# The last two experts behind the static norm, and one test of the list lengths where three were nested

## The chip, the cores and the metric

The kernel runs on one core of one Trainium2 chip. The metric is the device time of one launch in microseconds, from the core's first instruction to its last, as the median of several runs. Beside it stands one execution that the hardware profiler took; all rows of the trace come from that one, and its times count from the start of its span.

## The reference, cut

One decoder layer on 512 tokens of width 1024, in float32. Ahead of what matters here lie a layer norm, a mixer (differential attention and a gated short convolution) and a second norm. Then comes the part that the change touches: 32 experts, of which each token takes two of one group, and the last norm.

```python
def hier_moe(x, w_rg, b_rg, w_re, b_re, w1, w3, w2):
    ...                        # top-1 group, top-2 experts in it, gates
    def expert_block(args):
        xb, e = args
        return (jax.nn.silu(xb @ w1[e]) * (xb @ w3[e])) @ w2[e]
    ...                        # rows sorted by expert, padded, computed, gated
    return jnp.zeros_like(xt).at[tok].add(y).reshape(B, S, D)

# in reference(), after the mixer and its norm
ffn = hier_moe(h, w_rg[l], b_rg[l], w_re[l], b_re[l], w1[l], w3[l], w2[l])
h = layer_norm(DN_ALPHA * h + ffn, ln2_g[l], ln2_b[l])
```

## The kernel before, in words

Tokens lie in four blocks of 128 rows. `acc` (traced as `hres`) holds the four blocks of the sum that the last norm takes, 128 x 4 x 1024. The program goes through the 32 experts in a fixed order. For each of the first 30, `expert_flow(m)` multiplies the gathered rows of that expert with w1 and w3 (`up`, line 1158), applies silu on ScalarE (ACT) and the product on VectorE (DVE), turns the result (`turn`, line 1178 and 1179), multiplies with w2 (`down_products`, line 1191), scales with the gate, and adds the rows of the pair of experts before it to `acc` with selection products (`spread`, lines 1214 and 1216). Rows come in blocks of 32 slots: a first block of every expert is straight code, second to fourth blocks lie behind tests of the expert's count (`n_e`, lines 1339, 1358, 1366, 1374). The third and fourth block, "rest", lie far off the straight path, and `hint()` puts a branch hint for them on TensorE (PE), DVE and ACT behind the first block's products; their test has line 1366. Weights come through a ring of 17 places of 1 MB that SyncE (SP) fills in order (line 672); `place(k)` is the place of the k-th load.

The last two experts, lists of 64 slots at most, are not added to `acc` and normed with all else. The 512 tokens are normed without them ("static norm", written out by SP), and the rows of these two lists are normed a second time with their expert's part and written over the first by an indirect DMA from GpSimd (POOL). The steps by name:

- `summed_half(t, hf, both)` adds experts 28 and 29 to half a block of `acc` and sums it (L1528 on PE, L1530 on DVE); `spread_rows(k)` brings half a row of ln2's gain or shift to all partitions (L1499, copied by ACT, L1500); `squares(t, ...)` gives the variance (L1512, L1513); `rstds` the reciprocal root (L1517, L1518 on ACT, then five instructions on POOL, L1519 to L1523); `shifted_(t)` and `scaled_(t)` make the output rows (L1612, L1615), and SP writes them.
- `Slots(i, few)` is one list: `up`, `silu`, `gated`, `gather` (adds the rows of `acc` to the product's PSUM tile, L1568), `turn`, `down`, then `mean`, `rstd`, `norm` on the row pieces, and `write`. With `few` a list has 32 slots and each row lies in four pieces of 256, else 64 slots and two pieces of 512. `gains_of(n)` cuts ln2's rows to these pieces (L1505).
- `last_two(few, few_)` is the whole ending with both lists, written out four times: for each list in the short or the long form. `longest > 128` (line 1684, the crowded case) is tested first, then list 30 against 32 (line 1764), then list 31 against 32 (line 1765 or 1770). None of the three has a hint. Within `last_two` PE, DVE, ACT and POOL follow the order of the text, in which the sums and rows of the static norm stand between the two experts' products.

For these inputs no list is over 32 slots and none crowded: the trace shows the lines of the fourth copy, behind tests 1684, 1764 and 1770. What sets the order around the change is thus the text of `last_two`, the loads that SP issued up to 1254 us, and what the sequencer of each engine needs to get from the end of `expert_flow(29)` to that copy.

## Time and profile before

| what | value |
|---|---|
| time, median of 3 runs | 1298.69 us (1296.23 to 1305.65) |
| the profiled execution's own time | 1313.07 us |
| its span, first to last instruction | 1311.3 us |
| PE busy (weight loads apart) | 1099.6 us, 84% |
| DVE, ACT, POOL busy | 652.7, 434.2, 325.7 us |
| mean granted PE clock | 0.922 |
| last regular expert's last instruction (DVE) ends | 1254.7 us |
| first instruction of the last two experts on DVE, PE | 1272.1, 1273.4 us |
| last write to the output starts | 1305.2 us |

The page's row of 40 slices has PE at 9 tenths or near it up to the middle, and at 5 to 8 tenths through the experts; the last two slices, 33 us each, have 3 and 5 tenths of PE. The page's chain of waits follows only the last write and says nothing of the end; the timeline and the waits of the last 60 us do.

### The profile page before, as it was taken

Reading aid. Unit: us, or ns where it says so; the run is one execution under the profiler, and the core shown is the slowest. Engines: PE = TensorE matmul, PEld = TensorE weight load, DVE = VectorE, ACT = ScalarE, POOL = GpSimd, SP = SyncE. Lnnn points to the kernel's source line nnn. Section 1 sums busy time; section 2 is a strip of 40 time slices with the busy share of each in tenths; the row PEclk is TensorE's granted clock in tenths of the full one; section 3 lists DMA queues with packets and bytes.
Section 4 is the critical chain, followed back from the end, with each engine's and each line's share of the span. In section 5 each row is a group of like instructions: output and inputs, shape, how many; then the busy total and the mean of one; then the engine's idle time right before and its main releaser. Section 6 shows DMA issues by size and latency. Waiting matters only on the chain. (4 is left out here: it accounts for less than half of the span.)

```text
span 1311.3 us, 22649 instructions
## 1 busy us (share of the span) xinstructions
PE 1099.6 (84%) x8684; PEld 800.7 (61%) x8684; DVE 652.7 (50%) x1320; ACT 434.2 (33%) x953; POOL 325.7 (25%) x243
## 2 busy tenths in 40 slices
PE   7999999999999999998677778766776668787835
PEld 5887877877778888897445545444443445454513
DVE  7356666575666035538653444342454333445426
ACT  4444545455432223315221223121322112222214
POOL 3423333333235444425740201100000000000021
PEclk8999999999999999998798878888898887899968
DMA  6323222322264333584488946999645995685861
GB/s 186 94 74 103 65 79 88 85 70 67 73 175 128 89 83 95 191 322 180 183 329 363 390 169 254 377 366 372 248 194 205 380 400 209 251 352 232 319 254 73
DMA packets 127591, 267.73 MB, mean 204 GB/s; under 512 B 11745, under 2 KB 89930, under 8 KB 111023
## 3 DMA queue, kind: packets, MB, share of 16 engines
q1 hardware_dynamic: 117684, 254.72, 52.6%
q10 hardware_dynamic: 4666, 6.01, 1.4%
q0 software_dynamic: 5056, 4.50, 1.1%
q8 instruction: 121, 1.98, 0.7%
q14 instruction: 64, 0.52, 0.1%
HBM read 272.25 MB, written 4.52 MB: 211 GB/s over the span
## 5 line engine op out<-in xcount | busy, mean ns | idle before, releaser
L136 POOL TENSOR_TENSOR wl<-raw,wh 128x1024 fp32r<-128x1024 f32 x84 | 212.1, 2541 | 339.0 <-ACT wh L135 339.0
L1290 DVE TENSOR_TENSOR first<-p,first 64x256 f32<-64x256 f32 x49 | 20.9, 426 | 244.5 <-ACT first L1289 244.5
L135 ACT CAST wh<-raw 128x1024 fp32r<-128x1024 f32 x84 | 85.9, 1047 | 115.1 <-PE po L368 64.3
L1289 ACT ACTIVATE first<-p 64x256 f32<-64x256 f32 x49 | 18.5, 378 | 290.6 <-PE p L1158 282.3
L1284 DVE SCALAR_TENSOR_TENSOR ysb<-p,gts,ysb 32x256 fp32r<-32x256 f32 x164 | 78.7, 480 | 52.3 <-ACT ysb L1281 46.8
L1158 PE MATMUL p<-ring,xT 128*32 128x256 f32 x752 | 66.8, 461 | 38.4 <-PEq L1366 28.3
L1216 DVE TENSOR_TENSOR hres<-pc,hres 128x512 f32<-128x512 f32 x152 | 92.7, 680 | 6.4 <-PE pc L1214 3.5
L1281 ACT ACTIVATE ysb<-p,gts 32x256 fp32r<-32x256 f32 x164 | 76.5, 466 | 55.8 <-PE p L1191 52.4
L1078 POOL DMA_INDIRECT xgs<-h1d,idxs x15 | 15.4, 1026 | 316.7 <-PE px L1299 315.0
L1158 PE MATMUL p<-ring,first 128*32 128x256 f32 x896 | 66.6, 421 | 30.5 <-PEq L1366 22.0
L1158 PEld LDWEIGHTS p<-ring,xT 128*32 128x32 f32 x752 | 43.8, 131 | 55.6 <-issue 44.8
L1158 PEld LDWEIGHTS p<-ring,first 128*32 128x32 f32 x896 | 45.0, 120 | 47.8 <-issue 31.3
L1191 PE MATMUL p<-ring,first 128*32 128x256 f32 x944 | 59.9, 389 | 4.8 <-ACT first L1179 4.0
L1214 PE MATMUL pc<-ysb,sel 128*128 128x512 f32 x224 | 59.2, 406 | 0.5 <-PEq L1339 0.5
L921 PE MATMUL pd<-wh,mT 128*128 128x256 f32 x256 | 50.0, 296 | 1.2 <-DVE hres L927 1.2
L1158 PE MATMUL p<-ringraw,first 128*32 128x256 f32 x208 | 24.0, 484 | 32.1 <-DVE ysbr L1628 21.3
L368 PE MATMUL pg<-hTH,wh 128*128 128x512 f32 x128 | 50.7, 396 | 0.0
L368 PE MATMUL pg<-hTH,wl 128*128 128x512 f32 x128 | 50.5, 395 | 0.0
L368 PE MATMUL pg<-hTL,wh 128*128 128x512 f32 x128 | 50.5, 395 | 0.0
L457 ACT ACTIVATE e<-e,mn 128x128 f32<-128x128 f32 (+3 forms) x64 | 35.7, 558 | 40.2 <-DVE mn L454 40.0
L1214 PEld LDWEIGHTS pc<-ysb,sel 128*128 128x128 f32 x224 | 39.7, 188 | 14.9 <-issue 6.4
L1179 ACT COPY first<-ph 128x128 f32<-128x128 f32 x51 | 13.6, 266 | 101.7 <-PE ph L1178 101.5
(498 smaller groups left out, 2761.2 us busy)
## 6 DMA issues: line engine op xcount, KB each, us to landing
ring<-in_w_dram SPq DMA_DIRECT2D x114, 1024.0 KB, 11.5
raw<-in_w_in_dram SPq DMA_DIRECT2D x50, 512.0 KB, 4.4
ringwl<-in_w_dram SPq DMA_DIRECT2D x23, 1024.0 KB, 8.9
ringraw<-in_w_dram SPq DMA_DIRECT2D x22, 1024.0 KB, 9.0
ringwh<-in_w_dram SPq DMA_DIRECT2D x22, 1024.0 KB, 13.0
ringh<-in_w_dram SPq DMA_DIRECT2D x11, 1024.0 KB, 15.4
raw<-in_w_in_dram SPq DMA_DIRECT2D x7, 1024.0 KB, 5.5
raw<-in_w_attn_proj_dram SPq DMA_DIRECT2D x8, 512.0 KB, 5.5
```

The source lines that it names most:

```text
L135: A.copy(wh[:, ks], raw[:, ks])
L136: G.tensor_tensor(wl[:, ks], raw[:, ks], wh[:, ks].bitcast(F32), op=ALU.subtract)
L368: T.matmul(out_ps, l[:, k, c0:c0 + P], r[:, k, :], start=k == 0 and i == 0, stop=k == ND - 1 and i == 2)
L457: A.activation(e[:, :w], e[:, :w], AF.Exp, bias=mn[:], scale=-1.0, accum_out=sm)
L921: T.matmul(pds[n], mTs[t // 2][l][:, t % 2, k, :], r[:, k, :], start=k == 0 and i == 0, stop=k == ND - 1 and i == 2)
L1158: one = T.matmul(p1[m * g:m * g + m, 0:wd], xT[:, j, s0:s0 + m], (w1, w3)[2 * g // n][j][:, c0:c0 + wd], start=j == 0, stop=j == ND - 1)
L1191: T.matmul(o, l, r, start=j == 0 and not onto, stop=j == 3)
L1214: T.matmul(pc[:], sel[:, t * P:(t + 1) * P], ys[hf], start=i == 0, stop=i == len(parts) - 1)
L1216: added = V.tensor_tensor(at, pc[:], at, op=ALU.add)
L1281: high = A.activation(h, src, AF.Copy, scale=gc).ins
L1284: lows.append(V.scalar_tensor_tensor(l, src, gc, h.bitcast(F32), op0=ALU.mult, op1=ALU.subtract).ins)
L1290: turns["act"] = V.tensor_tensor(hh, p1[64:128, 0:256], hh, op=ALU.mult), one
```

## The change

The last two experts are written once, each list in blocks of 32 slots. `Slots(i, b)` is now block b of list i, always in four pieces of 256. The nested tests on each list's length go. The sums, spread rows, squares, rstd and gain copies of the static norm are taken out of `last_two`, put ahead of the crowded test and kept in the order of the text on PE, DVE and ACT; `sq` is one buffer of 1024 columns where there were two, and `ob` lies in other places. The crowded test stays and gets a hint, placed on PE behind the first sum's products, on DVE behind that sum, on ACT behind the copy of the rows. Behind it `last_two` does block 0 of both lists in an order of its own, and behind the last write one test (`longer > 32`) leads to block 1 of both. One of three values that were loaded into registers at m = 12 goes. The crowded case adapts (`spread_too`). In the diff below, lines of that case and repeated names are left out.

```diff
-    def expert_flow(m):
+    def expert_flow(m, spread_too=True):
...
-            V.tensor_copy(cmx[:, 1:3], last2)
+            V.tensor_copy(cmx[:, 1:2], mxf[:, 1:2])
...
-        for k, n in enumerate((4, 2)):
-            for g in range(n):
-                m = P // n
-                G.tensor_scalar(idx_[m * g:m * g + m, i, k:k + 1], token[0:m], float(n), float(g), op0=ALU.mult, op1=ALU.add)
+        for b in range(2):
+            for g in range(4):
+                G.tensor_scalar(idx_[32 * g:32 * g + 32, i, b:b + 1], token[32 * b:32 * b + 32], 4.0, float(g),
+                                op0=ALU.mult, op1=ALU.add)
...
-            longest, n_30, n_31 = (nc.values_load(cmx[0:1, i:i + 1], engines=every, min_val=0, max_val=2 * S)
-                                   for i in range(3))
-
-    in_order.__exit__(None, None, None)
+            longest, longer = (nc.values_load(cmx[0:1, i:i + 1], engines=every, min_val=0, max_val=2 * S)
+                               for i in range(2))
...
-    def gains_of(n):
...
+    def gains_of():
+        for g in range(4):
+            A.copy(gains[32 * g:32 * g + 32], g2[32 * g:32 * g + 32, :, 256 * g:256 * g + 256])
...
-        def __init__(self, i, few):
...
+        def __init__(self, i, b):
+            self.i, self.b, self.s0 = i, b, 64 * i + 32 * b
+            self.sel = onehots[:, i, :, 32 * b:32 * b + 32]
+            self.gc = gates_[:, i, b:b + 1]
...
-    ob = [spare_at[4 + t // 2][:, 1024 * (t % 2):1024 * (t % 2) + 1024] for t in range(NT)]
-    sq = spare_at[6]
+    by_hand = dict(engines={ENG.PE, ENG.DVE, ENG.Activation})
...
+    def last_two():
+
+        a_, b_ = Slots(0, 0), Slots(1, 0)
+        with tc.manual_schedule(**by_hand):
+            a_.up()
+            a_.silu()
+            a_.gated()
+            for t in range(NT):
+                shifted_(t)
+            a_.gather()
+            a_.turn()
+            a_.down()
+            b_.up(range(0, 4))
+            b_.gather()
+            exp_tables()
+            a_.mean()
+            a_.rstd()
+            A.preload_act_table_set("silu_and_others")
+            a_.norm()
+            scaled_(0)
+            scaled_(1)
+            b_.up(range(4, ND))
+            b_.silu()
+            b_.gated()
+            scaled_(2)
+            scaled_(3)
+            one = a_.write().ins
+            b_.turn()
+            exp_tables()
+            b_.down()
+            b_.mean()
+            b_.rstd()
+            b_.norm()
+            other = b_.write().ins
+            with tc.If(longer > 32):
+                for i in range(2):
+                    Slots(i, 1).all()
+        tc.declare_no_dep(other, one, reason="the two lists' rows differ")
+
+
+    ob = [place(6 * NE + 1)[:, 1024:2048], spare_at[3][:, 1024:2048]] + [xgs[:, t, :] for t in range(2)]
+    sq = place(6 * NE + 1)[:, 0:1024]
...
-    def last_two(few, few_):
...
-    with tc.If(longest > 128) as crowded:
+
+    copied = A.copy(rows2[0], rows_)
+    V.tensor_tensor(rows2[1], rows_, rows2[0].bitcast(F32), op=ALU.subtract)
+    for t in range(NT):
+        for hf in range(2):
+            added = summed_half(t, hf, both)
+            if t == 0 and hf == 0:
+                hint("crowded", (*added, copied))
+        if t in (0, 2):
+            spread_rows(t)
+            spread_rows(t + 1)
+        squares(t, sq)
+    exp_tables()
+    rstds(slice(0, NT))
+    A.preload_act_table_set("silu_and_others")
+    gains_of()
+    in_order.__exit__(None, None, None)
+
+    with tc.If(longest > 128, label="crowded") as crowded:
         fetch(xgr[:], NE - 1)
...
     with crowded.Else():
-        with tc.If(n_30 > 32) as many:
-            with tc.If(n_31 > 32) as many_:
-                last_two(False, False)
...
+        last_two()
```

Three places in the order of the instructions. ACT between the end of expert 29 and expert 31's silu: before, all of this stands behind the third test (L1770). `p_19118` and `p_19243` are the up products of experts 30 and 31, `first` the activations, `pg` a spread row, `ring_4534` ln2's rows, `hres` is `acc`, `ve` and `y_5587` variance and reciprocal root.

```order
L1627 CAST ysbr<-ring_4535 4x512
L1558 ACTIVATE first<-p_19118 64x256
L1500 COPY ring_4534<-pg 128x512 x2
L1513 ACTIVATE ringwh,ve<-hres,nmu 128x1024 x2
L1500 COPY ring_4534<-pg 128x512 x2
L55 ACT_TABLE_LOAD
L1513 ACTIVATE ringwh,ve<-hres,nmu 128x1024 x2
L1517 ACTIVATE y_5587<-ve,eps_17433 128x4
L1518 ACTIVATE y_5587<-y_5587 128x4
L1179 COPY first<-ph 128x128
L1656 ACT_TABLE_LOAD
L1505 COPY ring_4534<-ring_4534 32x512 x4
```

The same stretch of ACT now:

```order
L1665 CAST ysbr<-ring_4535 4x512
L1787 BRANCH_PREFETCH_HINT
L1494 COPY ring_4534<-pg 128x512 x2
L1506 ACTIVATE ring_4533,ve<-hres,nmu 128x1024 x2
L1494 COPY ring_4534<-pg 128x512 x2
L1506 ACTIVATE ring_4533,ve<-hres,nmu 128x1024 x2
L55 ACT_TABLE_LOAD
L1510 ACTIVATE y_5587<-ve,eps_17421 128x4
L1511 ACTIVATE y_5587<-y_5587 128x4
L1678 ACT_TABLE_LOAD
L1498 COPY ring_4534<-ring_4534 32x512 x4
L1682 COMPARE_AND_BRANCH
```

Expert 30's silu (L1558, now L1549) moved from the second place to behind the test, and all of the norm stands ahead of it. DVE behind the tests, from the last row means on; before, `p_19221` being the sum of expert 30's down product and gathered rows:

```order
L1512 TENSOR_SCALAR nmu<-sm 128x1 x2
L1612 SCALAR_TENSOR_TENSOR ringraw<-hres,nmu,ring_4534 128x1024 x4
L1615 SCALAR_TENSOR_TENSOR ringraw<-ringraw,y_5587,ring_4534 128x1024 x2
L1561 SCALAR_TENSOR_TENSOR first<-p_19243,ring_4535,first 64x256
L1615 SCALAR_TENSOR_TENSOR ringraw<-ringraw,y_5587,ring_4534 128x1024 x2
L1580 BN_STATS ring_4535<-p_19221 128x6
L1581 BN_AGGR ring_4535<-ring_4535 128x2
L1582 TENSOR_SCALAR ring_4535<-ring_4535 128x4
```

And now, from expert 30's gated product (L1552) on, `p_18473` being its up product and `p_18512` the sum of its down product and gathered rows:

```order
L1552 SCALAR_TENSOR_TENSOR first<-p_18473,ring_4535,first 64x256
L1658 SCALAR_TENSOR_TENSOR ring_4533<-hres,nmu,ring_4534 128x1024
L1658 SCALAR_TENSOR_TENSOR ring_4535<-hres,nmu,ring_4534 128x1024
L1658 SCALAR_TENSOR_TENSOR xgs<-hres,nmu,ring_4534 128x1024 x2
L1584 BN_STATS ring_4535<-p_18512 128x6
L1585 BN_AGGR ring_4535<-ring_4535 128x2
L1586 TENSOR_SCALAR ring_4535<-ring_4535 128x4
L1591 BN_STATS ring_4535<-pm 128x6
L1592 BN_AGGR ring_4535<-ring_4535 128x2
L1593 TENSOR_SCALAR ring_4535<-pm,ring_4535 128x1
L1594 SCALAR_TENSOR_TENSOR ring_4535<-p_18512,ring_4535,ring_4534 128x256
```

Expert 30's gated product now stands ahead of the shifted rows, with no sums between, and its statistics and norm follow them at once; before, they stood behind all four scaled rows (L1615), which now come later (L1661). POOL at the program's end, before:

```order
L1519 TENSOR_SCALAR ve<-ve 128x4
L1520 TENSOR_TENSOR u_5588<-ve,y_5587 128x4
L1521 TENSOR_TENSOR u_5588<-u_5588,y_5587 128x4
L1522 TENSOR_SCALAR u_5588<-u_5588 128x4
L1523 TENSOR_TENSOR y_5587<-u_5588,y_5587 128x4
L1604 DMA out_dram<-ring_4535,idx 2048x256 x2
L1770 UNCONDITIONAL_BRANCH
```

And now, from the crowded case's end on:

```order
L1682 UNCONDITIONAL_BRANCH
L1607 DMA out_dram<-ring_4535,idx 2048x256 x2
L1648 COMPARE_AND_BRANCH
L1607 DMA out_dram<-ring_4535,idx 2048x256 x2
L1648 UNCONDITIONAL_BRANCH
```

The rstd instructions moved ahead of the crowded test, and a test stands behind the two writes, over two more.

## Rows read from the trace of the kernel before

**Rows 1.** Waits of 1252 to 1274 us: who waited for whom, total us, times, longest us

```profile
DVE ysbr L1628 <- issue: 17.4, 1, 17.4
...
ACT ysbr L1627 <- issue: 9.0, 1, 9.0
```

**Rows 2.** Stretches: length, busy us per engine (instructions), PE clock, DMA share, GB/s

```profile
1254.86:1272.09 17.23, 0.00 (x0) 0.00 (x0) 0.00 (x0) 0.62 (x1) 5.33 (x17) 0.55 0.71 268
1273.30:1276.80 3.50, 3.43 (x36) 1.84 (x39) 0.00 (x0) 0.00 (x0) 0.00 (x0) 0.50 0.02 5
```

**Rows 3.** Lines of the three tests: ns min/median/max, first and last start us

```profile
L1684 PEldq COMPARE_BRANCH  x1: 7241/7241/7241, 1253.2 to 1253.2; - x1
...
L1764 ACTq COMPARE_BRANCH  x1: 57/57/57, 1257.6 to 1257.6; - x1
...
L1764 DVEq COMPARE_BRANCH  x1: 71/71/71, 1261.2 to 1261.2; - x1
...
L1770 ACTq COMPARE_BRANCH  x1: 45/45/45, 1262.6 to 1262.6; - x1
...
L1770 DVEq COMPARE_BRANCH  x1: 56/56/56, 1267.6 to 1267.6; - x1
```

**Rows 4.** DMA, 1256 to 1264 (packets, MB, share), and issues from 1245 on

```profile
q8 instruction: 4, 0.07, 6.3%
...
ring<-in_w_dram SPq DMA_DIRECT2D x5, 1024.0 KB, 16.9
```

**Rows 5.** Line 1366 (columns as rows 3), and the whole run's waits behind it

```profile
L1366 PEldq COMPARE_BRANCH  x35: 77/468/5582, 642.8 to 1252.5; - x35
...
PE p L1158 <- PEq L1366: 63.7, 15, 7.5
...
ACT first L1289 <- DVEq L1366: 2.4, 3, 0.8
```

**Rows 6.** Timeline of PE: start us, us, instruction, count, idle before

```profile
1273.37 3.64 PE L1158 MATMUL p<-ringraw,first 128*32 128x256 f32 x32 [21.26 <-DVE ysbr L1628]
...
1277.41 1.20 PE L1528 MATMUL pc<-ysb,sel 128*128 128x512 f32 x4
...
1291.21 1.91 PE L1158 MATMUL p<-ring,first 128*32 128x256 f32 x32
```

**Rows 7.** Timeline of ACT

```profile
1281.87 1.08 ACT L1500 COPY ring<-pg 128x512 f32<-128x512 f32 x2 [1.38 <-PE pg L1499]
1282.86 1.15 ACT L1513 ACTIVATE ringwh<-hres,nmu 128x1024 f32<-128x1024 f32 x1
...
1286.69 1.28 ACT L55 ACT_TABLE_LOAD   x1
...
1292.39 2.54 ACT L1505 COPY ring<-ring 32x512 f32<-32x512 f32 x4
```

**Rows 8.** Timeline of DVE

```profile
1286.80 4.87 DVE L1612 SCALAR_TENSOR_TENSOR ringraw<-hres,nmu,ring 128x1024 f32<-128x1024 f32 x4
...
1295.82 2.47 DVE L1615 SCALAR_TENSOR_TENSOR ringraw<-ringraw,y,ring 128x1024 f32<-128x1024 f32 x2
1298.32 0.43 DVE L1580 BATCH_NORM_STATS2 ring<-p 128x6 f32<-128x256 f32 x1
...
1299.77 0.17 DVE L1588 BATCH_NORM_STATS2 ring<-pm 128x6 f32<-128x4 f32 x1 [0.54 <-PE pm L1584]
...
1302.68 0.16 DVE L1588 BATCH_NORM_STATS2 ring<-pm 128x6 f32<-128x4 f32 x1
...
1304.40 0.48 DVE L1601 SCALAR_TENSOR_TENSOR ring<-ring,ring 128x256 f32<-128x256 f32 x1
```

**Rows 9.** Timeline of POOL, and its drains at the end (line 1798)

```profile
1303.06 1.12 POOL L1604 DMA_INDIRECT out_dram<-ring,idx  x1 [10.19 <-DVE ring L1589]
1305.17 0.97 POOL L1604 DMA_INDIRECT out_dram<-ring,idx  x1 [0.99 <-POOLq L1684]
...
L1798 POOLq DRAIN  x3: 46/105/5135, 1305.3 to 1311.0; - x3
```

192 lines of the change are left out of this document (61 added, 131 removed).

## The prediction

> **What bounds the kernel now.** I read the views from the end backwards. The waits of 1252 to 1274 us come first: between the last regular expert and the last two, DVE waits 17.4 us and ACT 9.0, and the view says "issue", that is, for nothing that it knows of [rows 1]. The stretches say the same: from 1254.86 to 1272.09 PE and DVE do nothing and ACT 0.62 us, while DMA moves 268 GB/s [rows 2]. Then the lines of the three tests (1684, 1764, 1770): every engine takes three jumps in a row. DVE leaves the last expert at 1254.9, takes the second test at 1261.2, the third at 1267.6, and works at 1272.1: 6.3, 6.4 and 4.5 us each. On PE the record of the first test itself lasts 7.24 us. ACT takes the second at 1257.6 and the third at 1262.6, 5.0 us apart, and works 0.5 us behind that [rows 3]. In the middle of it the instruction queue moves packets, on DMA engines that are busy with weights [rows 4]. So I read each long jump as a wait for instructions.
>
> Against these stand the skips of a "rest" block, which every expert makes with a branch hint ahead (line 1366). PE's test takes 77 to 5582 ns there, median 468, and PE's experts waited for it for 63.7 us, in 15 waits; for DVE's test of that line another engine waited three times, 0.8 us at most [rows 5]. Reading: a hinted jump is cheap on DVE, and a lottery on PE.
>
> [...] From DVE's first instruction (1272.1) to the start of the last write (1305.2) are 33.1 us.
>
> **The change, part by part.** It takes out two of three nested tests, moves the sums, squares and rstd of the static norm ahead of the test that stays, and hints that one. I follow the path from 1254.9, when DVE has left the last expert.
>
> (a) Ahead of the test. ACT's order now ends in four copies, four squares, table load, Ln and Exp, table load, four gain copies, test. Its first copy needs two sums from PE, 1.2 us for the four products [rows 6], and one spread row, half of that again: it starts at about 1256.8. ACT then owes 2 x 1.08 + 4 x 1.15 + 0.2 + 2 x 1.28 + 2.54 [rows 7], and Ln and Exp, rounded to 0.5: 12.6 us. It waits some 0.6 us for the second pair of sums: the test at about 1270.0. PE (16 products for sums, 8 for rows, 24 x 0.3 = 7.2 us) is through at 1262, DVE at 1262.7. POOL's five instructions of rstd and its two register loads follow Exp; they are needed only by the scaling at 1280.
>
> (b) The test. ACT's hint is issued at about 1255, 15 us ahead. I price its jump at 0.3 us, below the 0.5 of its third jump; the other end is its second, unhinted and far, 5.0 us [rows 3]. PE's jump costs 0.1 to 5.6 us [rows 5], 7.2 unhinted. PE then has expert 30's up products (3.8 us) and its gather (1.9) to do and is not waited for until 1271.2, so 3.5 us of its jump are hidden, and the median is free. DVE's lies between 1262.7 and 1269.1 at worst and is hidden.
>
> (c) Behind it, expert 30: silu 0.4, gated 0.5, and with handovers 1271.2. Now two rails. DVE does the four shifted instructions, 4.87 us [rows 8], to 1276.1. PE turns and ACT copies (0.75 with handovers), then down, half of expert 31's up and its gather, 32 products each, 3 x 1.91 [rows 6]: 1277.7, and the mean's product 0.4: 1278.1. PE's rail ends last. Before, the sums and spread rows lay between the up products; laid end to end this costs some us that the old order did not pay, and they are in these clock times.
>
> (d) From the mean's product on: statistics of the product to the end of the normalised row took 1302.68 to 1304.88, 2.2 us [rows 8]. So 1280.3; two scaled rows, half of 4.87: 1282.7; gated 0.5; two scaled rows: 1285.7. Beside those PE turns and does expert 31's down, until about 1286.0. Its mean with the product took 1298.32 to 1299.77, 1.45 [rows 8]: 1287.4, norm 2.2: 1289.6; the last write starts 0.3 later, 1289.9. The first write waits until all four row blocks have landed. Before, the last scaled row ended at 1298.3 [rows 8] and the first write started 4.8 us later at the most, named as released by DVE [rows 9]; the same 4.8 behind 1285.7 would be 1290.5, with 1.12 us of issue 1291.6. That is the upper end, 1.7 us; I take none of it, since DVE and not a DMA was the releaser.
>
> (e) Behind the last write POOL, and every engine, takes the new test. POOL skips two instructions; I take 0.5 us, ACT's jump to nearby code [rows 3]. The other end is a far jump, 4.5 us. POOL's closing drain lasts 5.1 us behind the write [rows 9]; PE, whose skipped blocks are long, reaches the test at 1287.4 and DVE at 1289.6, so their jumps lie beside that drain.
>
> (f) Small parts, at nothing: one register load less on each engine at expert 12, far ahead of any stall; two index instructions more for each list on POOL and shorter gates and averages, all in POOL's idle time. The weights of expert 31 are issued until 1254.0 and land 16.9 us later [rows 4], 1270.9; its up starts at 1273.9, its down at 1284: no wait, and 3 us of cover. SP's order does not change.
>
> (g) Clock. PE now waits some 2.7 us ahead of 1271 and 3 us ahead of 1283. If that costs nothing, the sum is as above; if both restarts go as the one after the old stall, 2 x 1.73 us more [rows 6]. PE was idle 17 us there and about 3 here; I take 1.0.
>
> Sum: the last write moves from 1305.2 to 1289.9, 15.3 us; less 0.5 for (e) and 1.0 for (g): 13.8 us gained. The profiled execution of 1313.07 us (span 1311.3) would become 1299.3. That execution is 14.4 us above the median of the runs, and no wait at the end is peculiar to a profile that I can see, so I take the 13.8 off the median: 1298.69 - 13.8 = 1284.9. One per cent, about what a measurement of this kernel can tell from no change, is 13.0 us, 1285.7: the forecast lies on that edge.
>
> **Rivals.** *The hint brings nothing (0.17).* The jump that stays then costs ACT 5.0 us instead of 0.3, all of it on the path: 1289.6. For it: PE's skips of up to 5.6 us in spite of a hint, and weights on the DMA engines until about 1271. Against it: DVE's hinted skips, and a lead of 15 us. [...]
>
> *The stall is smaller outside the profile (0.15).* DVE's third jump, with the weight traffic nearly over, cost 4.5 us; three at that price are 13.5 instead of 17.2, and the gain shrinks by 3.7: 1288.6. For it: the profile is 1.1% slow. Against it: the traffic that the fetches share is the weights', and those are there in every run.
>
> *The last test lies on the path (0.06).* POOL's jump behind the write is a far one, and its drain begins only after it: 4.5 us instead of 0.5, 1288.9.
>
> *Slower (0.04).* One mechanism: the code moved. From expert 12 on every stream is some instructions shorter, and whether PE's hinted skip at line 1366 costs 0.5 or 5 us may change with where it lies against the fetched blocks. Some ten of these skips follow. Each that turns costs about 4.7 us; three eat the gain, six give 1313. For it: the spread of 77 to 5582 ns. Against it: skips may as well turn the other way, and the shift is a handful of instructions.
>
> *It doesn't do what it says:* one list would have to hold more than 32 rows, so that second blocks run. The trace shows 128x256 statistics for both lists [rows 8], which is the short form, so the inputs take the short way; no chance of its own.
>
> **How the numbers follow.** The forecast, hints that work on ACT and DVE, has 0.58, with a range of its own of 1280 to 1289: 1.0 down and 2.5 up for (g), 1.7 up for the landing, and 2 to 4 us down for handovers and tables that may overlap better than end to end. The range for 8 in 10 takes in the next two rivals, and a little below because the timed runs scatter by 9 us: 1278 to 1291. Faster by over 1% needs 1285.7: somewhat over half of the forecast's range and some scatter of the rest, 0.51. Within 1%: what is left of it and the three mild rivals, 0.45. Slower: 0.04.
>
> **What would show it.** In the changed profile: no "issue" wait above 1 us on DVE ahead of the first sum; sums from 1255 on, and PE's clock at full speed there; silu within 0.5 us behind ACT's gain copies; DVE idle for some 8 us ahead of gated; the last write 35 us behind the last expert. I am wrong in (b) if 3 us or more stand between gain copies and silu; in (e) if the drain starts more than 1 us behind the write; in (c) and (d) if a rail is over 2 us longer than here; and in the whole if PE's waits for the test at line 1366 add up to much more or less than 63.7 us.

## The result, and the profile after

The changed kernel takes 1291.51 us in the median of ten runs (1285.53 to 1296.66), the kernel before 1300.84 in the ten that were timed beside it. The ratio is 0.9928, with a 95% interval of 0.9902 to 0.9955: 9.3 us less, 0.7%, where 13.8 us were forecast. The forecast of 1284.9 and its range (up to 1291) lie below it, the upper end by half a microsecond.

| profiled execution | before | after |
|---|---|---|
| its own time; span (us) | 1313.07; 1311.3 | 1295.01; 1293.2 |
| mean granted PE clock | 0.922 | 0.917 |
| last regular expert ends on DVE (D) | 1254.7 | 1244.9 |
| from D to the last write | 50.5 | 41.0 (forecast 35.2) |
| from the last write to the span's end | 6.1 | 7.3 (forecast 6.6) |
| sum of both | 56.6 | 48.3 |

D lies 9.8 us earlier in this execution, with the same code ahead of it but for a few instructions. That is how far two executions differ, and no gain: a run below with all code ahead of D as before (e5) has D at 1244.1. The change acts behind D, and there it saves 56.6 - 48.3 = 8.3 us, in line with the 9.3 of the medians. So times below are told from D, written "D + ...".

The wait of 17.4 us "for nothing" [rows 1] is gone. What stands in its place, PE first; columns as in [rows 6]:

```profile
1245.17 1.82 PE L1521 MATMUL pc<-ysb,sel 128*128 128x512 f32 x4 [2.82 <-DVEq L1366]
1246.92 2.07 PE L1493 MATMUL pg<-ysbr,identr 4*128 4x512 f32 x4
1248.92 3.67 PE L1521 MATMUL pc<-ysb,sel 128*128 128x512 f32 x8
1252.52 1.18 PE L1493 MATMUL pg<-ysbr,identr 4*128 4x512 f32 x4
1253.63 1.19 PE L1521 MATMUL pc<-ysb,sel 128*128 128x512 f32 x4
1258.13 3.64 PE L1158 MATMUL p<-ringraw,first 128*32 128x256 f32 x32 [3.31 <-ACT ring L1506]
...
1271.93 1.93 PE L1158 MATMUL p<-ring,first 128*32 128x256 f32 x32
1277.22 0.47 PE L1178 MATMUL ph<-cpk,first 64*128 64x64 f32 x2 [3.35 <-DVE first L1552]
1278.05 3.64 PE L1191 MATMUL p<-ring,first 128*32 128x256 f32 x32 [0.35 <-ACT first L1179]
```

Four products of the sums took 1.20 us before [rows 6]; now the first sixteen products take 1.8 to 2.1 for four. Expert 30's first products take 3.64, as they did behind the old stall, and expert 31's down 3.64 as well. The granted clock in the three places (length, busy us per engine with PE first, PE clock, DMA share, GB/s):

```profile
1245.17:1252.50 7.33, 7.33 (x16) 4.60 (x16) 4.34 (x12) 3.36 (x6) 4.70 (x15) 0.53 1.01 408
...
1258.13:1261.78 3.65, 3.65 (x36) 2.00 (x40) 0.00 (x0) 3.55 (x7) 1.00 (x5) 0.50 0.03 9
1271.93:1273.85 1.92, 1.92 (x33) 0.94 (x32) 1.52 (x8) 1.09 (x3) 0.00 (x0) 1.00 0.05 9
1278.05:1281.70 3.65, 3.64 (x32) 1.38 (x32) 1.50 (x2) 1.24 (x1) 0.00 (x0) 0.50 0.92 374
```

At 0.50 the 32 products take 3.64 us, at 1.00 they take 1.93. PE had waited 2.8, 3.3 and 3.4 us ahead of the three slow stretches. The crowded test (line 1682 now), as [rows 3]:

```profile
L1682 PEldq COMPARE_BRANCH  x1: 6179/6179/6179, 1251.8 to 1251.8; - x1
L1682 DVEq COMPARE_BRANCH  x1: 69/69/69, 1255.8 to 1255.8; - x1
L1682 ACTq COMPARE_BRANCH  x1: 55/55/55, 1260.5 to 1260.5; - x1
```

PE's jump took 6.18 us in spite of its hint, issued 6.6 us ahead. PE had products queued until 1254.8, so 3.3 us of the jump are idle. (The view names ACT's squares, L1506, as the releaser of expert 30's products; without the far jump, in e2 below, they start at D + 8.4, ahead of the last squares.) Then ACT and DVE, on the way to expert 30:

```profile
1260.45 2.50 ACT L1498 COPY ring<-ring 32x512 f32<-32x512 f32 x4
1264.08 0.38 ACT L1549 ACTIVATE first<-p 64x256 f32<-64x256 f32 x1 [1.13 <-PE p L1158]
```

```profile
1264.64 0.48 DVE L1552 SCALAR_TENSOR_TENSOR first<-p,ring,first 64x256 f32<-64x256 f32 x1 [8.68 <-ACT first L1549]
```

The gain copies end at 1262.95 (D + 18.0) and silu waits another 1.13 us, for PE's products: PE is the late one, not ACT's jump. Two things make it late, the idle part of its jump and the half clock behind it. DVE idles 8.68 us, as foreseen. At the end, POOL:

```profile
1283.16 1.11 POOL L1607 DMA_INDIRECT out_dram<-ring,idx  x1 [22.83 <-DVE ring L1586]
1285.91 0.97 POOL L1607 DMA_INDIRECT out_dram<-ring,idx  x1 [1.63 <-DVEq L1648]
```

```profile
L1648 POOLq INC_SWDGE_SEM  x1: 1250/1250/1250, 1285.9 to 1285.9; - x1
...
L1787 POOLq DRAIN  x3: 46/99/5017, 1287.4 to 1292.9; - x3
```

The test on POOL is short (45 ns), but the skipped block leaves an adjustment of 1.25 us behind it, and the drain of 5.0 us starts 1.47 us after the last write; before it was 0.16 [rows 9]. PE's waits for line 1366 add up to 66.0 us, against 63.7 [rows 5], so the "moved code" played no part.

### The profile page after: what moved, and what is told of

The parts are those of the page before. It is cut to its first block, busy times and chain, and to the rows that moved or that the text cites. A ratio compares the mean times of both kernels' runs of the same rounds, so it can differ in the third digit from the quotient of the medians.

```text
span 1293.2 us, 22646 instructions
## 1 busy us (share of the span) xinstructions
PE 1101.6 (85%) x8684; PEld 801.6 (62%) x8684; DVE 653.6 (51%) x1320; ACT 436.8 (34%) x955; POOL 324.8 (25%) x246
## 5 line engine op out<-in xcount | busy, mean ns | idle before, releaser
L1158 PE MATMUL p<-ring,first 128*32 128x256 f32 x896 | 69.6, 440 | 32.2 <-PEq L1366 23.9
L1078 POOL DMA_INDIRECT xgs<-h1d,idxs x15 | 15.4, 1024 | 314.5 <-PE px L1299 311.3
L1191 PE MATMUL p<-ring,first 128*32 128x256 f32 x944 | 61.6, 399 | 4.2 <-ACT first L1179 4.0
L368 PE MATMUL pg<-hTL,wh 128*128 128x512 f32 x128 | 50.5, 395 | 0.0
L368 PE MATMUL pg<-hTH,wl 128*128 128x512 f32 x128 | 50.5, 395 | 0.0
L457 ACT ACTIVATE e<-e,mn 128x128 f32<-128x128 f32 (+3 forms) x64 | 35.7, 558 | 40.3 <-DVE mn L454 40.1
L1214 PEld LDWEIGHTS pc<-ysb,sel 128*128 128x128 f32 x224 | 39.7, 188 | 14.9 <-issue 6.4
L1078 POOL DMA_INDIRECT xgr<-h1d,idxs x15 | 15.7, 1048 | 120.7 <-PEq L1366 60.6
```

The lines of the kernel that those rows point to most:

```text
L368: T.matmul(out_ps, l[:, k, c0:c0 + P], r[:, k, :], start=k == 0 and i == 0, stop=k == ND - 1 and i == 2)
L457: A.activation(e[:, :w], e[:, :w], AF.Exp, bias=mn[:], scale=-1.0, accum_out=sm)
L1078: G.indirect_dma_start(out=out, out_offset=None, in_=h1d[:], in_offset=bass.IndirectOffsetOnAxis(ap=idxs[:, c:c + 1], axis=0), bounds_chec ...
L1158: one = T.matmul(p1[m * g:m * g + m, 0:wd], xT[:, j, s0:s0 + m], (w1, w3)[2 * g // n][j][:, c0:c0 + wd], start=j == 0, stop=j == ND - 1)
L1191: T.matmul(o, l, r, start=j == 0 and not onto, stop=j == 3)
L1214: T.matmul(pc[:], sel[:, t * P:(t + 1) * P], ys[hf], start=i == 0, stop=i == len(parts) - 1)
```

## The experiments

All are the changed kernel with one edit, unless said otherwise. Last write and tail are read as in the table above, each from the run's own profile; the ratio is to the kernel before in the same series. The times can't tell 3 us from nothing, since D alone lies between 1236.0 and 1254.7 us in the profiles of the table; the distances can, as those of the changed kernel, of the runs without a hint, with the early hint and with the last write moved agree (41.0 in all four). But each distance is of one execution, and where PE's clock falls otherwise, the same code can differ by 1 to 2 us, as shown below.

| run | D to last write | tail | sum | ratio, 95% interval |
|---|---|---|---|---|
| before | 50.5 | 6.1 | 56.6 | 1 |
| changed | 41.0 | 7.3 | 48.3 | 0.9928 (0.9902 to 0.9955) |
| e1 no hint | 41.0 | 6.6 | 47.6 | 0.9920 (0.9895 to 0.9944) |
| e11 early hint | 41.0 | 7.1 | 48.2 | 0.9938 (0.9917 to 0.9958) |
| e2 branches exchanged | 39.4 | 8.0 | 47.4 | 0.9923 (0.9895 to 0.9952) |
| e3 products ahead of turn | 39.7 | 6.1 | 45.8 | 0.9895 (0.9866 to 0.9923) |
| e4 write behind test | 41.0 | 6.3 | 47.2 | 0.9916 (0.9881 to 0.9951) |
| e6 products ahead of sums | 40.1 | 7.0 | 47.1 | 0.9897 (0.9861 to 0.9932) |
| e7 shifted rows first | 38.9 | 6.8 | 45.7 | 0.9918 (0.9892 to 0.9944) |
| e12 new order, mended | 34.9 | 7.2 | 42.1 | 0.9887 (0.9867 to 0.9907) |
| e5 before, one test | 37.6 | 6.2 | 43.7 | 0.9890 (0.9850 to 0.9929) |
| e10 old order, last test | 39.5 | 6.5 | 46.0 | 0.9916 (0.9886 to 0.9946) |
| e9 old order, exchanged | 30.0 | 7.0 | 37.0 | 0.9877 (0.9846 to 0.9908) |

My theory on reading the result: PE holds the path, by its jump and by a clock that falls in each wait. Rivals: ACT's chain ahead of the test, the last test, the new order itself.

**Does the hint do anything?**

```diff
-            if t == 0 and hf == 0:
-                hint("crowded", (*added, copied))
...
-    with tc.If(longest > 128, label="crowded") as crowded:
+    with tc.If(longest > 128) as crowded:
```

> The changed kernel without the branch hint for the crowded test; all else is the same. In the changed kernel's trace the record of PE's hinted jump lasts 6.18 us, DVE works again 3.04 us behind its test, ACT's sequencer is through its test within 0.6 us, and 41.0 us lie between the end of the last regular expert (DVE) and the start of the last write. Theory 1 (the hint works on ACT and DVE and does little for PE): ACT's jump goes to about 5.0 us, of which 2.5 us lie beside its gain copies, so silu starts about 1.4 us later; DVE's goes to about 6.3 us and stays hidden; PE's to 7.2 us. The distance grows by 1 to 1.5 us, to about 42.3. Rival (the hint brings nothing on any engine): jumps and distance as with it, 41.0 within 0.5. Second rival (the three engines' fetches hinder each other as they did before the change): ACT and PE both wait 7 us or more, distance 44 or more. In time the first means 0.1%, below what these rounds separate; the trace decides.

```profile
L1680 PEldq COMPARE_BRANCH  x1: 6139/6139/6139, 1244.4 to 1244.4; - x1
```

The rival holds: nothing changes that reaches the path. PE's jump lasts 6.14 us, DVE gets to the wait behind its test 2.8 us later (3.0 with the hint), ACT's jump lies beside its gain copies in both, and the distance is 41.0. So the step that the prediction took from line 1366 had no ground for this test. Was the hint too late? Here it stands in the last regular expert, behind the hint for "rest":

```diff
         hint(f"rest{m}", (turns["up"], *turns["act"]))
+        if m == NE - 3:
+            hint("crowded", (turns["up"], *turns["act"]))
```

> The changed kernel with the hint for the crowded test put behind the hint for the block 'rest' in the last regular expert, some 17 us ahead of the test on PE instead of 6.6. Without the hints for line 1366 PE's skips there rose from 66 to 119 us in all while DVE's and ACT's stayed, so a hint can help PE; the shortest lead of those was 8.5 us. Theory 1 (the crowded hint came too late): PE's jump falls from 6.2 us to 0.5 or less, its up starts right behind ACT's squares, silu stands within 0.2 us behind the gain copies, 39.5 to 40 us to the last write instead of 41.0. Rival (one hint is held at a time, or the test between drops it): PE's jump stays at 6 us, and the skip of line 1366 ahead of it, 0.44 us in every run so far, goes to 3 us or more. Second rival (a hint of this distance does nothing): jump 6 us, skip 0.44.

```profile
L1682 PEldq COMPARE_BRANCH  x1: 6164/6164/6164, 1246.7 to 1246.7; - x1
```

6.16 us: it doesn't help earlier either, and the skip of line 1366 ahead of it took 0.79 us instead of 0.44, far from the 3 us or more of the rival. And do hints help at line 1366 at all? All are taken out:

```diff
-        hint(f"rest{m}", (turns["up"], *turns["act"]))
...
-        with tc.If(n_e > 1, label=f"rest{m}"):
+        with tc.If(n_e > 1):
```

> The changed kernel without any branch hint: neither for the crowded test, where taking it away changed no jump (PE 6.14 us without, 6.18 with), nor for the blocks 'rest' of line 1366, which every one of the 30 regular experts skips. The prediction took from the skips of line 1366 that a hint makes a jump cheap (0.5 us on DVE, median 0.47 us on PE). Theory 1 (the hints bring nothing anywhere; the skips are short for another reason): PE's waits for line 1366 stay at 60 to 70 us in all, its skips keep their spread from 0.1 to 5.6 us, DVE's stay at 0.5, the time stays within 3 us of the changed kernel's. Rival (hints work for these skips and only the one for the crowded test came to nothing): PE's skips go to 4 us or more each, its waits to 120 us or more, DVE's skips to 3 us, and the time is 40 us or more above the changed kernel's.

Line 1366 is 1365 there:

```profile
L1365 PEldq COMPARE_BRANCH  x35: 67/3492/7047, 640.9 to 1290.1; - x35
...
L1365 DVEq COMPARE_BRANCH  x35: 43/56/63, 645.7 to 1291.8; - x35
...
PE p L1158 <- PEq L1365: 97.5, 18, 7.9
```

The time is 1348.43 us, 57 more than the changed kernel's in its own series (ratio to before 1.035, against 0.993). On PE these hints work: the median goes from 0.47 to 3.49 us, the 35 records from 66 to 119 us in all, and expert products' waits for them from 66.0 to 97.5. On DVE nothing changes: from the starts of its 35 tests to its next records are 14.6 us in all without hints and 15.1 with. DVE's cheap skips, on which the prediction built, are cheap without a hint. What sets the crowded test apart on PE might be the length of what is jumped over. Two runs, timed and profiled once each, cut the crowded case to 100 rows on PE, where it has 568 and "rest" 122 up to its first jump; they leave out the rest of that case, which these inputs don't enter:

```diff
     with tc.If(longest > 128, label="crowded") as crowded:
-        fetch(xgr[:], NE - 1)
...
+        for m in (NE - 2, NE - 1):
+            w1, w3, w2 = weights(m)
+            hT = turn(act32(up(True, xTs[1], 0, w1, w3), 0), 2)
+            down_block(hT, w2, yss[0], gc0[0:32], 0)()
```

> The changed kernel with a crowded case that is cut short, so that its code on PE has 100 rows instead of 568 (the block 'rest' of line 1366 has 122, which its hint helps); it leaves out the rest of the crowded case, which these inputs don't enter. Hint and place as in the changed kernel. Theory 1 (the length of what is jumped over decides whether a hint helps): PE's jump falls from 6.2 us to 0.5 or less, silu stands right behind the gain copies, the last write comes at 39.5 to 40 us behind the last regular expert instead of 41.0. Rival (a hint at this place does nothing at any length, since so few instructions lie between hint and test, or a later hint than that of the block 'rest' isn't taken): PE's jump is as long as in the twin without a hint, 3 to 6 us. Second rival (short jumps need no hint): under 1 us in both.

> The same without the hint; it too leaves out most of the crowded case. Without hints the skips of line 1366, of like length, took 3 to 6 us on PE in 23 of 35. Theory 1 (length decides whether a hint helps): 3 to 6 us on PE, against 0.5 or less with the hint. Rival (a hint at this place does nothing): the same as with it, within 0.5 us. Second rival (short jumps need no hint): under 1 us in both.

With the hint, then without:

```profile
L1682 PEldq COMPARE_BRANCH  x1: 6187/6187/6187, 1249.7 to 1249.7; - x1
```

```profile
L1680 PEldq COMPARE_BRANCH  x1: 6514/6514/6514, 1249.7 to 1249.7; - x1
```

Length isn't it for PE: 6.2 and 6.5 us, and the last write comes at D + 41.15 with the hint, not at 39.5 to 40, and at 40.64 without. (DVE's jump, though, is 0.2 us in both, where the whole crowded case cost 2.8 to 3.0.) Nor is 6 us fixed: PE's jump over the whole case took 3.1 us in e6 below, with the hint, and 3.6 in the run without any hint, where the weights had nearly all landed (DMA at 30 GB/s in its first half and at 0 in its second, where it was at 400 in the first two thirds of the changed kernel's). Why a hint shortens PE's skips at line 1366 and not this one stays open.

**What is the far jump worth?** Without hint, and with the branches exchanged, so that the common case is the next code:

```diff
-    with tc.If(longest > 128, label="crowded") as crowded:
+    with tc.If(longest < 129) as few:
+        last_two()
+    with few.Else():
         fetch(xgr[:], NE - 1)
...
-    with crowded.Else():
-        last_two()
```

> The changed kernel without hint and with the two branches exchanged: the last two experts follow the test as the next code, and the crowded case stands behind them, so that every engine jumps only at the very end, over the crowded code. Theory 1 (PE's jump holds up the path): no far jump is left ahead of expert 30. PE's up starts about 0.5 us behind the last squares' buffers instead of 3.3 us later, silu follows the gain copies within 0.2 us instead of 1.13 us; the distance from the last regular expert to the last write is 41.0 less 1 to 1.5, about 39.7. At the end POOL's jump over the crowded code stands between the write and its drain: 0.2 us if it is near, up to 4.5 us if it has to be fetched, so the time is between 1 us less and 3 us more than that of the changed kernel. Rival (ACT's chain ahead of the test sets silu alone): distance 41.0 within 0.5, since silu can't start before the gain copies end. Second rival (what holds PE is not the test but the buffers or the weights): PE's up starts as late as with the jump, at 13 us behind the last regular expert.

```profile
L1680 PEldq COMPARE_BRANCH  x1: 81/81/81, 1250.0 to 1250.0; - x1
```

```profile
1258.64 2.49 ACT L1498 COPY ring<-ring 32x512 f32<-32x512 f32 x4
1261.16 0.38 ACT L1549 ACTIVATE first<-p 64x256 f32<-64x256 f32 x1
```

PE's jump falls from 6.2 to 0.08 us and silu follows the gain copies at once. It comes 2.5 us earlier: 1.1 is what PE held up by its jump and the half clock behind it (the first 32 up products take 1.93 us here), and 1.4 is ACT's chain, which ended at D + 16.6 although nothing in it was changed. At the last write 1.6 us of this arrive (39.4 instead of 41.0), since expert 30's down ran at half clock this time (1.94 us for its first 16 products, 1.07 in the changed kernel). The far jump now stands at the very end; PE's took 4.7 us there, beside the drain (4.67 in e9, which ends alike), and the tail is 0.7 us longer. What moved ACT's chain is the clock: the stretch of 9.65 us from the first sum (about D + 0.25), in this run, in the changed kernel and in the run with the short crowded case and hint:

```profile
1244.76:1254.41 9.65, 9.65 (x52) 6.08 (x56) 6.86 (x21) 6.46 (x12) 5.18 (x16) 0.82 1.00 407
```

```profile
1245.17:1254.82 9.65, 9.65 (x24) 5.93 (x24) 5.76 (x17) 5.68 (x10) 4.70 (x15) 0.65 1.01 409
```

```profile
1243.68:1253.33 9.65, 9.65 (x22) 6.18 (x23) 5.33 (x16) 5.46 (x10) 4.72 (x15) 0.56 1.01 409
```

At a clock of 0.82 the gain copies end at D + 16.6, at 0.65 at D + 18.0 (the same in e1, e4, e7 and e11, all at 0.65), at 0.56 at D + 19.15 (so too in e3). The stretch of e2 ends with some of expert 30's products; over the same 24 products of sums and rows alone it is 8.3 us at 0.79 in e2, 9.65 at 0.65 in the changed kernel, 10.9 at 0.55 in e13, and 6.8 at 1.00 in e6 below. From the first sum to the end of the gain copies are 16.4, 17.8, 18.9 and 15.1 us: the same instructions, in step with the clock.

**Can PE be kept at full clock?** Four products whose results go nowhere, in PE's wait ahead of expert 31's turn, or ahead of the first sum:

```diff
             b_.up(range(4, ND))
+            warm(4, cpk[:, 0:384])
```

> The changed kernel with four products of an identity with 384 columns put on PE behind expert 31's second half of up, where PE waits 3.35 us for expert 31's gated product; their results go nowhere. Theory 1 (the clock falls in that wait and makes expert 31's down products slow): turn and down run at full clock, down 1.9 instead of 3.64 us, the granted clock of that stretch rises from near 0.5 to near 1.0, the last write comes 1.7 us earlier (distance 39.3 instead of 41.0). Rival (down is slow for its weights or its PSUM, not for the clock): down stays at 3.6 us, distance 41.0 or more, as the dummies may delay the turn. Second rival (the wait ends later by something else, DVE's scaled rows): down is faster but DVE's statistics are not earlier, because DVE is busy until 2.2 us ahead of them: then only up to 2.2 us can be gained, which bounds the first too.

```profile
1268.33 0.34 PE L1178 MATMUL ph<-cpk,first 64*128 64x64 f32 x2 [0.57 <-DVE first L1552]
1269.02 1.93 PE L1191 MATMUL p<-ring,first 128*32 128x256 f32 x32 [0.35 <-ACT first L1179]
```

```profile
1274.26 1.11 POOL L1607 DMA_INDIRECT out_dram<-ring,idx  x1 [21.71 <-DVE ring L1603]
1275.68 0.97 POOL L1607 DMA_INDIRECT out_dram<-ring,idx  x1 [0.31 <-issue]
```

Silu stands at D + 19.2 as in the changed kernel, so all behind it can be compared. Down takes 1.93 instead of 3.64 us: the clock it was. The last write gains 1.3 of the 1.7 us; then it stands right behind the first, which comes at D + 38.2 as before. The first has to wait until the static rows have landed; the view names DVE, whose row ended long before, but SP issued the last of these rows at 1270.7, and they land 2.7 to 3.0 us after their issue (in the changed kernel the last of them is issued at 1279.15, and its traffic ends at 1281.9). The third rail, which the prediction priced as an upper end, is thus 0.4 us behind.

```diff
+    warm(4, cpk[:, 0:384])
     copied = A.copy(rows2[0], rows_)
```

> The changed kernel with four products of an identity with 384 columns on PE ahead of the first sum, where PE waits 2.8 us for the last regular expert's rows; their results go nowhere. In the changed kernel's trace the first 16 products of sums and rows run at 1.8 to 2.1 us for four, the last eight at 1.2. Theory 1 (the clock falls in that wait): all run at 1.2, ACT's gain copies end 1.5 to 2.5 us earlier than 18.0 us behind the last regular expert, PE reaches its test earlier by as much, silu follows at 17 to 17.7 instead of 19.2, the last write at 39 to 39.7 instead of 41.0. Rival (the sums wait for DVE's adds, 0.7 us for each half, and for ACT's copies of rows): products are faster and the chain is not, 40.5 or more. Second rival (the clock doesn't depend on what PE did just before): products as slow as without, 41.0 or more.

```profile
1239.80 2.85 PE L992 MATMUL spare<-cpk 128*128 128x384 f32 x8 [2.82 <-DVEq L1366]
```

The clock of the sums is 1.00 (6.8 us for the 24 products), but the dummies don't run in the wait. The row shows them held by the same wait for DVE's skip of line 1366; they start where the first sum did, and the sums start 2.4 us late. So the gain copies end at D + 17.8, where 18.0 was, though from the first sum on they need 15.1 us instead of 17.8. What it gained (0.9 us to the last write) came from PE, whose jump lasted 3.1 us in this run and whose up products ran at full clock (1.93 us for the first 32), so that silu follows the copies at once. The forecast of 1.3 to 2 us took the wait for one that dummies can fill.

**DVE's idle time.** Shifted rows ahead of gated, and on PE expert 30's mean product ahead of expert 31's gathering:

```diff
-            a_.gated()
             for t in range(NT):
                 shifted_(t)
+            a_.gated()
...
-            b_.gather()
             exp_tables()
             a_.mean()
+            b_.gather()
```

> The changed kernel with the four shifted row blocks ahead of expert 30's gated product on DVE instead of behind it, and expert 30's mean product ahead of expert 31's gathering on PE. DVE idles 8.7 us ahead of gated, and the shifted rows need 4.9 us and only values that are there 11 us behind the last regular expert. Theory 1 (behind silu DVE is a rail of the end, as the prediction's sum has it): expert 30's statistics start at 23 instead of 25.0, its norm ends at 27.5 instead of 29.3, the scaled rows end some 3 us earlier, expert 31's gated product comes at about 30 instead of 31.7, PE's wait ahead of it is 1.5 us instead of 3.35, and the last write is 1.7 to 3.4 us earlier (37.6 to 39.3 instead of 41.0). Rival (PE's rail sets the end): the mean's product waits for PE, gated moves by less than 0.5, 40.5 or more. Second rival (DVE's late start of shifted was cover for the landing of the static rows): the first write is not earlier than 38.2, which holds the last one at 39.6.

38.9 instead of 41.0, within the forecast: expert 30's statistics start at D + 23.4 (25.0 before). But the edit moves two things, and which of them gained isn't shown. In the changed kernel the statistics end at 1270.92, and the mean's product still waits until PE is through with the gathering:

```profile
1269.78 1.91 PE L1559 MATMUL p<-hres,ring 128*32 128x256 f32 x32
1271.62 0.39 PE L1588 MATMUL pm<-ring 128*128 128x6 f32 x2
```

By these rows, an estimate, earlier statistics alone would have brought nothing at that product, and an earlier place of it alone 0.7 us at most. The two together brought 1.7 us (D + 25.0 instead of 26.7). PE's wait ahead of expert 31's turn shrinks to 1.6 us, and its down is still slow (3.62 us). One thing was not foreseen: POOL's instructions of rstd, 0.2 us each in the changed kernel, take 1.1 while DVE works on the shifted rows, and 0.2 again behind them (DVE ends at 1260.1):

```profile
1259.07 1.10 POOL L1515 TENSOR_SCALAR u<-u 128x4 f32<-128x4 f32 x1
1260.26 0.20 POOL L1516 TENSOR_TENSOR y<-u,y 128x4 f32<-128x4 f32 x1
```

**The last test.** The last write moved behind it:

```diff
-            other = b_.write().ins
             with tc.If(longer > 32):
...
+            other = b_.write().ins
```

> The changed kernel with the last write (expert 31's rows) behind the last test instead of ahead of it; the skipped second blocks stand ahead of that write. In the changed kernel POOL's closing drain starts 1.47 us behind the start of the last write, since the not taken block leaves POOL an adjustment of 1.25 us; before the change it was 0.16 us. Theory 1 (the tail grew by that adjustment): the test and the adjustment now lie in POOL's wait for expert 31's norm, the drain starts 0.2 us behind the write, and from the write to the span's end go 6.1 instead of 7.3 us; distance to the last write 41.0 within 0.5; 1.2 us less in all. Rival (the drain's start is set by the write itself, or the write now waits for all engines' tests): the tail stays at 7.3 us, or the last write comes up to 4 us later because PE's jump of 3.9 us ends only then.

As theory 1 has it: 41.0 to the last write, and the drain starts 0.06 us ahead of it instead of 1.47 behind. The tail is 6.3 instead of 7.3 us; it also varies with the drain's own length (5.5 us here, 5.0 in the changed kernel, 4.3 in e1), so the size of this gain is known to about 1 us only.

**The order itself.** The kernel before, with the two tests of the list lengths taken out; it leaves out lists of over 32 rows, which these inputs don't have:

```diff
     with crowded.Else():
-        with tc.If(n_30 > 32) as many:
...
-                last_two(True, True)
+        last_two(True, True)
```

> The kernel before with the two tests of the list lengths taken out, so that only the crowded test (without a hint) stands ahead of the last two experts; their order, with sums and spread rows between the products, is the old one. It leaves out lists of 33 to 64 rows, which these inputs don't have. Before the change three jumps in a row took 17.2 us on DVE, and 33.1 us lay between DVE's first instruction behind them and the last write; 50.5 us in all from the last regular expert. Theory 1 (each jump costs its 4 to 7 us on every engine, and they add): DVE starts its first sum 6.3 us behind the last regular expert instead of 17.4, the distance to the last write is 50.5 less 10.9, about 39.6, and the time is about 11 us less than before; the change's new order with the norm ahead of the test then brought nothing, or lost 1.4 us (41.0). Rival (the order brings part): the first jump alone costs more, as PE's lasts 7.2 us and its cold products follow, the distance is 43 or more, and the new order is worth 2 us or more. Second rival (the tests overlap): distance 47 or more.

```profile
L1684 PEldq COMPARE_BRANCH  x1: 7001/7001/7001, 1242.6 to 1242.6; - x1
```

```profile
1249.87 3.53 PE L1158 MATMUL p<-ringraw,first 128*32 128x256 f32 x32 [8.34 <-DMA ring<-in_w_dram]
1253.76 1.19 PE L1528 MATMUL pc<-ysb,sel 128*128 128x512 f32 x4
```

37.6 us to the last write: 12.9 us less than before, more than the 10.9 that I had worked out, and 3.4 less than the changed kernel, with a whole unhinted jump of 7.0 us on PE and 6.3 on DVE in it. Taking two tests out brings 12.9 us (PE's first product moves from D + 18.7 to 5.8, DVE's first instruction, which I had counted by, from 17.4 to 7.0); by these two profiles all else in the change gives 4.6 of them back, tail included. The times don't separate the two (their intervals overlap). A likely reason is in the second row: in the old order the sums stand behind 40 of the 64 products that the trace counts for expert 30's up, and run at full clock (1.19 for four); ACT's squares and copies lie beside PE's products of both experts. To see whether the blocks of 32 slots or the last test had a part in it, the old order with these:

```diff
     def last_two():
...
+            A.copy(rows2[0], rows_)
+            V.tensor_tensor(rows2[1], rows_, rows2[0].bitcast(F32), op=ALU.subtract)
+            a_.up(range(0, 5))
+            summed_half(0, 0, both)
...
-    copied = A.copy(rows2[0], rows_)
...
-    gains_of()
```

> The same kernel as the one with exchanged branches and old order, but with the branches as in the changed kernel and no hint: the crowded test ends in a far jump, and the norm stands behind it, between the products. Against the changed kernel only the order differs (and a hint that was seen to do nothing); against the kernel before with one test only the short blocks and the last test. Theory 1 (the move of the norm ahead of the test is what the change loses): 37.5 us to the last write, tail 6.3 to 7.3, 44 to 45 us in all, 3.5 us less than the changed kernel's 48.3. Rival (the blocks of 32 or the last test lose it): 40 us or more to the last write. Second rival (the gain of the old order was peculiar to that run): within 1 us of 41.0.

39.5 and 46.0: between the theory and the rival. It beats the changed kernel by 2.3 us in all, and stays 1.9 behind its sibling on the way to the last write. PE's jump was 0.8 us longer (7.76 against 7.00), and the sums that follow had a clock of 0.83 against 1.00:

```profile
1253.76:1263.85 10.09, 10.09 (x85) 5.69 (x82) 7.04 (x22) 5.64 (x10) 0.00 (x0) 1.00 0.19 74
```

```profile
1254.97:1266.95 11.98, 11.98 (x85) 6.54 (x82) 8.09 (x23) 7.14 (x11) 0.00 (x0) 0.83 0.09 35
```

(the first is of the run with one test, the second of this one; the same work, 1.9 us longer; 0.8 of both is made up later). So the new order loses 1.5 to 3.4 us to the last write against the old, by one execution of each; what part of it the short blocks and the last test have isn't separated. Then the old order with exchanged branches:

> The changed kernel's parts (blocks of 32 slots, one test behind the last write) in the order of the kernel before (sums, spread rows and squares between the two experts' products, all behind the crowded test), no hint, and the branches exchanged so that the last two experts are the next code and the crowded case stands behind them. The old order behind one far jump needed 37.55 us from the last regular expert to the last write, of which the jump is 6.3 us on DVE and 7.1 on PE. Theory 1 (the new order lost time and the jump is a pure stall): 37.55 less 6 to 8, since PE's up needs nothing of the last regular expert and can start ahead of its end: last write at 29.5 to 31.5. The tail is 7 to 8 us, as with the exchanged branches before (7.99); from the last regular expert to the span's end 37 to 39.5 us, against 48.3 of the changed kernel and 56.6 before: about 10 us less time than the changed kernel. Rival (weights hold it: expert 31's last load lands 17 us behind its issue): PE's up of expert 31 waits for a DMA, last write at 33 to 36. Second rival (PE's jump over the crowded code at the end is longer than POOL's drain): tail 9 us or more.

```profile
L1689 PEldq COMPARE_BRANCH  x1: 81/81/81, 1239.8 to 1239.8; - x1
```

```profile
1240.14 1.93 PE L1158 MATMUL p<-ringraw,first 128*32 128x256 f32 x32 [1.42 <-DVE ysb L1284]
...
1242.44 1.21 PE L1521 MATMUL pc<-ysb,sel 128*128 128x512 f32 x4
```

30.0 to the last write, 37.0 in all, as forecast: PE starts expert 30 ahead of D (1241.3 in this run), at full clock, and no jump stands in its way. In time it is 1283.35 us, 16 less than before. Against e10, which differs by the branches alone, the sum is 9.0 us less. Last, the new order with all single repairs: exchanged branches, both sets of dummies, shifted rows first and last write behind the test, each as shown above, and the gain copies later:

```diff
     A.preload_act_table_set("silu_and_others")
-    gains_of()
...
             a_.turn()
+            gains_of()
             a_.down()
```

> The changed kernel's order, mended where the single runs showed a loss: branches exchanged (silu 16.65 us behind the last regular expert instead of 19.2), dummies ahead of the sums and ahead of expert 31's turn, shifted rows ahead of gated, gain copies (2.5 us) behind expert 30's turn on ACT, the last write behind the last test. Theory 1 (these losses are separate and add): silu at 12.5 to 14, 18.5 us from there to the last write instead of 21.8, last write at 31 to 33, tail 6.3 to 8. Rival (ACT's chain of squares and the two table loads ahead of the test sets everything): silu no earlier than 15, last write at 34 or more, so that the old order behind exchanged branches, forecast at 29.5 to 31.5, is better however the new one is mended. Second rival (the landing of the static rows holds the first write): first write no earlier than 36.

Silu comes at D + 15.3, not at 12.5 to 14, and the last write at 34.9, not at 31 to 33. The rival's numbers hold: silu waits for ACT's squares, Ln, Exp and two table loads, which the new order puts ahead of it. But 2.4 us of that are the dummies, which here too start at the end of PE's wait; without that delay silu might have come at 12.9 (an estimate), within theory 1. So e12, 4.8 us behind e9 to the last write, doesn't show how far the new order could be mended. By the distances the old order with exchanged branches is the best of all. By time it is faster than the kernel before, but its interval overlaps that of the changed kernel, and the medians of e3, e12 and e9 (1283.96, 1283.83, 1283.35 us) tell none of the three apart.

## Why the prediction came out wrong

The main reading held: the old stall was three jumps. With two taken out the last write comes 12.9 us earlier (e5), and in the changed kernel nothing is left of DVE's wait of 17.4 us. What failed is the size of what the new code puts in its place. Forecast from D to the last write: 35.2 us; measured 41.0. The 5.8 us come from three steps (2.7, 0.8 and 2.2 by rounded numbers).

**Step (a), 2.7 us.** The gain copies were to end by D + 15.3 and ended at 18.0. The work was counted rightly (12.6 us on ACT); mis-sized were the waits for PE's sums, which I took at full clock "1.2 us for the four products" and which ran at 0.53. Full clock was read off sums that stood behind other products, and the change puts them behind a wait of 2.8 us. Other runs of the same code ended between 16.6 and 19.15, by the clock; e6, at 1.00, needed 15.1 us from the first sum on, which from D + 0.25 would have been the 15.3 of the forecast. I also forecast "PE's clock at full speed there" as a sign, and this sign failed first.

**Step (b), 0.8 us.** The failed step is "a hinted jump is cheap on DVE, and a lottery on PE". The crowded hint brought nothing that reached the path (e1, e11), and DVE's skips were cheap without a hint (e8: 14.6 us for 35, 15.1 with). On PE the hint did nothing for the crowded test (6.18 us with it, 6.14 without), while at line 1366 the hints are worth 57 us of the run. The price of the step was small, since the jump lay mostly beside other work: 1.1 us held up silu. That took the jump's idle 3.3 us and the half clock behind it together (3.64 instead of 1.93 us for the first 32 up products, a restart that the sum hadn't at this place); in e2 and e6 both were smaller or gone, and no run takes away one alone. ACT, on which the rival "the hint brings nothing" put its 5 us, had its jump beside the gain copies: in e3, and in e8 without any hint, silu follows them without a gap, 2.5 us behind the test. That rival, at 1289.6, was nearest to the time and had the right fact; but its 4.7 us weren't on ACT, so that its number is near is luck.

**Steps (c), (d) and (g), 2.2 us.** From silu to the last write I had 19.6 us (with no restart in it), measured 21.8. Expert 31's down at half clock alone is 1.7 of it, and e3 got 1.3 of that back. I did name the restarts ("2 x 1.73", the 3.64 us behind the old stall less the 1.91 of the same form later) and took 1.0 for the two, because PE "was idle 17 us there and about 3 here". A wait of 3.3 us cost as much as that of 17 (3.64 us for the 32 products behind either). A third restart, that of the sums, wasn't on the list. The rest is the turn and the mean's product of expert 31, slower too (0.47 us, where 0.34 was before, and 0.56, as before, where expert 30's had 0.36). Up to expert 31's turn the two rails were as forecast: PE's ended last, with the mean's product at 1271.6, and DVE's last scaled rows ended 15.5 us behind silu, where the sum has 15.4. The sign set for (c) and (d), a rail over 2 us longer, thus came true, for PE's clock.

**Step (e), 0.7 us.** The tail grew by 1.2 where 0.5 was forecast (0.5 to 1.2 in e1, e11 and the changed kernel, which have the same end). POOL's jump is near, as said; the adjustment of 1.25 us wasn't known, and the sign that I had set ("the drain starts more than 1 us behind the write") came true with 1.47. The rival with a far jump on POOL (4.5 us) fell.

Together 2.7 + 0.8 + 2.2 + 0.7, less the 1.0 already taken for (g), are 5.4 of the 5.5 us between 13.8 and the 8.3 of the profile. Right were: DVE idle for some 8 us (8.7), no wait for weights, the near test on POOL, the waits of line 1366 unmoved, the short form for both lists, and that the gain outside the profile is that inside it (9.3 and 8.3).

One larger omission: I compared the new order only with the old stall, never with the old order behind one test. The sum had the sentence "laid end to end this costs some us that the old order did not pay"; had I worked it out, 50.5 less two of DVE's three jumps (10.9 us by [rows 3]) would have given 39.6 for the old order beside 35.2 for the new. So the whole move rested on 4.4 us, and it put four engines' work in line behind PE's sums, whose clock I had not looked at.

## What to carry to other kernels

A duration that is read from products behind other products need not hold behind a wait: here four took 1.2 us behind others and 1.8 to 2.1 behind a wait of 2.8 us. Where a change puts products behind such a wait, both clock levels that the trace shows (0.50 and 1.00) belong in the sum. Ahead of a test whose common case jumps far, look first whether the branches can be exchanged: by the profiles this was worth 9.0 us in the old order (e10 against e9), and 0.9 in the new one (e2), where the jump lay beside other work. And where work is moved to fill a stall, price the same code with the stall removed and the work left in place.
